# Feed-forward inner layer in two groups of tiles, x kept on chip at every post norm, other weight buffers, more layers in halves at the seams

## The chip, the cores and the metric

One core of a Trainium2 chip runs the whole network once. The metric is the device time of one execution in microseconds (us); lower is better. A time is the median of several runs.

## What is computed

x has 512 tokens of 1024 features. Four feed-forward layers, two attention-like mixers and two more mixers change it in turn, in the order feed-forward 0, attention, feed-forward 1, feed-forward 2, mLSTM, feed-forward 3, the even mixer, the odd mixer, and a last norm. Around the first six of these stand a norm before and a norm after (with a factor 0.5 in the gain of the feed-forwards' second norm):

```python
def _rms_norm(x, g):
    y = x * lax.rsqrt(jnp.mean(x * x, axis=-1, keepdims=True) + EPS)
    return y * g
def _swiglu(x, w_gate, w_up, w_down):
    return (jax.nn.silu(x @ w_gate) * (x @ w_up)) @ w_down
# feed-forward, D_FF = 2816:   x = x + 0.5 * _rms_norm(_swiglu(_rms_norm(x, g_pre), ...), g_post)
# attention and mLSTM:         x = x + _rms_norm(mixer(_rms_norm(x, g_pre)), g_post)
```

All of it is float32.

## The kernel before

**Layout and products.** Features lie on the partitions, tokens along the columns: x is 8 tiles of 128x512 (`k.x`). A float32 product is made of three products of reduced float32 (`mm3`, L287 to L289): each operand is split in a high and a low part, and low weights by high x, high weights by low x and high by high are added up in one PSUM bank. The three lines take a third of the matmuls each. `k.xs` holds the split x, which norm factors `rb` multiply later, behind the product.

**Weights.** `wload` (L260) brings a weight tile `wt` by DMA (128x1024, 512 KB), ScalarE makes the high part `wh` (L267, a cast), and VectorE the low part `wl` (L268, a subtraction); where `eng` is given, GpSimd does the subtraction. Each of the three has 4 buffers.

**Layers.** A `Lin` makes 128 output features for all 512 tokens. A feed-forward has 22 gate and 22 up layers (24 matmuls each), whose results become `hh` and `hl`, the 22 tiles of the inner layer, and then 8 down layers of 66 matmuls, for which all 22 tiles are on chip.

**Seams.** Between two parts of the network the norm needs every feature of a token. So the last layers of a part (`ntail`) and the first of the next one (`nfront`) run in two halves of 256 columns (`halves`, L316): the first half of the tokens goes through the post norm, the residual sum and the split while TensorE works on the second half of the last layers, and the second half while TensorE works on the first half of the next part. In the tail the second half goes backwards over its layers, and `tkeep` layers keep their weights; others are loaded twice. A tail's half is 2 layers in a feed-forward, 3 in the others; the front is 4 layers.

**The chain of a post norm** (`PostNorm`, L477 to L513). Of each layer ScalarE writes the squares to `ew` and the product times the gain to `hf`, which lies in the memory of x itself; GpSimd, for the last layer VectorE, adds the squares to `acc` (L493). Then two small matmuls sum over the partitions (L372), VectorE scales (`rsv`, L391), GpSimd takes the power -0.5 (L392), two small matmuls spread the result (L380), and for each of 8 tiles VectorE multiplies (L508) and adds the old x (L512, tiles 2 and 5 on GpSimd). The old x was copied to DRAM (`keep_x`, L465) and comes back by 8 DMAs for each half (L510). Behind it stand the split for the next part (ScalarE L433, VectorE L434), the squares of the new x (ScalarE L415, sums on GpSimd and VectorE L417, L419) and their column sums, scale, power and spread (`rc`), which give `rb`.

**What sets the order.** Chains are generators: `tick` advances them after so many matmul triples, so TensorE's place for each small matmul is fixed by numbers (`yield 3`, `lag=26`, 4 and 6 in `rsqrt_mean`); the tile scheduler then orders each engine's queue when the program is built. SP issues the DMAs in order. `ssm_prep` is side work for the even mixer that is spread over the gate and up layers of feed-forward 3; it begins with two DMAs into `pdt` (L1066) and an exponential on it (L1068).

Of the kernel before, what the change touches and what calls it, by code (L numbers as in the profile page):

```python
# [9 lines left out]
F32 = mybir.dt.float32  # L10
# [454 lines left out]
def keep_x(k):  # L465

    old = k.dram.tile([KX, P, T], F32, name="old", tag="old")
    for i in range(KX):
        k.nc.sync.dma_start(old[i], k.x[i])
    return old  # L470


class PostNorm:
# [3 lines left out]
    def __init__(s, k, gain, old):  # L477
        s.k, s.gain, s.hf, s.old = k, gain, hf_views(k.x), old
# [23 lines left out]
    def chain(s, c0, c1, then):  # L502
# [13 lines left out]
def ffn(k, w, gpost, side=None, begin=None):  # L516
# [3 lines left out]
    NB = 10  # L520
    with k.phase("ffn") as pool, k.psum("ffn_ps", True), ExitStack() as late:
        xs = k.xs
        hs = [(pool.tile([P, T], R, name=f"hh{i}"), pool.tile([P, T], R, name=f"hl{i}")) for i in range(NF - NB)]
# [24 lines left out]
        n1 = 2 * (NF - NB)  # L548
        if begin:
# [73 lines left out]
def attn(k):  # L623
# [3 lines left out]
    with k.phase("attn") as pool, k.psum("attn_ps") as pp:  # L627
# [9 lines left out]
        zero = pool.tile([P, T], F32, name="zero")  # L637
# [12 lines left out]
        def project(a, i):  # L650
# [26 lines left out]
            lins = [Lin(k, [(A["aqk"][2 * a + j, i], KX)], xs, ev, nc.gpsimd) for j, ev in ((1, ev_k), (0, ev_q))]  # L677
            if (a, i) != (0, 0):
                run_lins(lins)
            else:  # L680
# [4 lines left out]
                lin_tok(k, A["av"][0], xs, ev_v(0), nc.gpsimd)  # L685
# [76 lines left out]
        old = keep_x(k)  # L762
# [11 lines left out]
        post = PostNorm(k, k.vec(3), old)  # L774
        run_lins([Lin(k, [(A["ao"][m], KX)], ys, post.evac(m)) for m in range(KX)], ntail=3, on_half=post.finish)
# [5 lines left out]
def mlstm(k):  # L781
# [6 lines left out]
    with k.phase("mlstm") as pool, k.psum("mlstm_ps") as pp, ExitStack() as late:  # L788
# [11 lines left out]
        def gates(pa):  # L800
# [215 lines left out]
        post = PostNorm(k, k.vec(9), old)  # L1016
        run_lins([Lin(k, [(A["mo"][m], KX)], ys, post.evac(m)) for m in range(KX)], ntail=3, on_half=post.finish)
# [202 lines left out]
def even(k):  # L1220
# [3 lines left out]
    with k.phase("even") as pool, k.psum("even_ps") as pp:  # L1224
        xs, rb = k.xs, k.rb
        pwt = pool.tile([P, 4, P], F32, name="pwt")
        nc.sync.dma_start(pwt, A["pw"])
# [127 lines left out]
        for n, l in enumerate([None] + lus[2:] + lz[2:6] + lup + lz[6:], 1):  # L1355
# [237 lines left out]
```

## Time and profile before

| what | value |
|---|---|
| median of 3 runs | 2586.77 us (2586.46 to 2589.38) |
| the profiled execution's own time | 2588.2 us |
| its span, first to last instruction | 2586.4 us |
| its mean granted TensorE clock | 0.984 |
| busy: TensorE, VectorE, ScalarE, GpSimd | 95%, 53%, 39%, 25% |

The profile is one execution. TensorE's busy time is the sum of the time in which some matmul was under way; matmuls overlap each other, so their listed durations are longer than their steps from start to start. The granted clock is the share of TensorE's full clock that the chip let through.

### The profile page before, as it was taken

To read this page: it belongs to the slowest core of one execution; us is meant where nothing else is said; L and a number is where in the kernel's file an instruction comes from. 1 tells how busy PE (TensorE), PEld (TensorE's weight loads), DVE (VectorE), ACT (ScalarE), POOL (GpSimd) and SP (SyncE) were. 2 spreads that over 40 slices of the span, in tenths; PEclk is the share of its full clock that TensorE was granted. 3 is DMA by queue.
4 is the path that set the end of the run, shared out by engine and by line. 5 is a ranking of instruction groups with operands and counts; after the bars stand their busy time and mean duration, and the time that the engine had idled before them with its cause. 6 is when DMAs were issued, how large, how long until landed. Compare 5 with 4: busy or idle time off the path is not lost. (4 is left out here: it accounts for less than half of the span.)

```text
span 2586.4 us, 33337 instructions
## 1 busy us (share of the span) xinstructions
PE 2466.2 (95%) x12864; PEld 2071.5 (80%) x12864; DVE 1358.1 (53%) x2292; ACT 997.0 (39%) x1656; POOL 643.3 (25%) x566
## 2 busy tenths in 40 slices
PE   8999989999999999999999899979999999999898
PEld 7888887677888888888888788867888888787677
DVE  5443246656544432644422657449973245856884
ACT  4222234446522222422222445433232232346662
POOL 2111025030311100211100353122211014217961
PEclk9999999999999999999999999999999999999998
DMA  5223336122432333422233422224443347231111
GB/s 168 95 98 94 93 102 196 50 86 66 140 105 98 98 90 104 155 98 98 93 92 98 151 82 74 82 87 144 144 157 94 96 135 227 79 117 66 66 58 50
DMA packets 105679, 273.12 MB, mean 106 GB/s; under 512 B 17920, under 2 KB 39040, under 8 KB 105008
## 3 DMA queue, kind: packets, MB, share of 16 engines
q1 hardware_dynamic: 105520, 270.99, 33.1%
q8 instruction: 101, 1.65, 0.3%
q14 instruction: 58, 0.48, 0.1%
HBM read 243.66 MB, written 23.09 MB: 103 GB/s over the span
## 5 line engine op out<-in xcount | busy, mean ns | idle before, releaser
L287 PE MATMUL pa<-xs,wl 128*128 128x512 f32 (+1 forms) x2368 | 882.5, 373 | 9.2 <-DVE wl L268 7.1
L288 PE MATMUL pa<-xs,wh 128*128 128x512 f32 (+1 forms) x2368 | 881.7, 372 | 5.3 <-DVE xs L434 4.6
L289 PE MATMUL pa<-xs,wh 128*128 128x512 f32 (+1 forms) x2368 | 877.7, 371 | 0.0
L267 ACT CAST wh<-wt 128x1024 fp32r<-128x1024 f32 (+2 forms) x423 | 432.5, 1023 | 1048.8 <-issue 610.4
L268 DVE TENSOR_TENSOR wl<-wt,wh 128x1024 fp32r<-128x1024 f32 (+2 forms) x371 | 450.4, 1216 | 455.4 <-ACT wh L267 454.3
L287 PEld LDWEIGHTS pa<-xs,wl 128*128 128x128 f32 x2368 | 448.8, 190 | 87.4 <-ACT sq L415 7.1
L288 PEld LDWEIGHTS pa<-xs,wh 128*128 128x128 f32 x2368 | 448.5, 189 | 81.6 <-DVE xs L434 6.0
L289 PEld LDWEIGHTS pa<-xs,wh 128*128 128x128 f32 x2368 | 448.9, 190 | 74.3 <-issue 1.8
L533 POOL TENSOR_TENSOR ew<-ew,rb 128x512 f32<-128x512 f32 (+1 forms) x96 | 160.4, 1672 | 712.4 <-ACT ew L532 712.4
L287 PE MATMUL pa<-hh,wl 128*128 128x512 f32 (+1 forms) x880 | 311.6, 354 | 13.6 <-DVE wl L268 13.6
L288 PE MATMUL pa<-hl,wh 128*128 128x512 f32 (+1 forms) x880 | 309.6, 352 | 0.0
L289 PE MATMUL pa<-hh,wh 128*128 128x512 f32 (+1 forms) x880 | 309.6, 352 | 0.0
L287 PEld LDWEIGHTS pa<-hh,wl 128*128 128x128 f32 x880 | 167.6, 190 | 38.9 <-DVE wl L268 14.7
L493 POOL TENSOR_TENSOR acc<-acc,ew 128x512 f32<-128x512 f32 (+1 forms) x44 | 51.6, 1172 | 546.6 <-ACT ew L488 546.6
L288 PEld LDWEIGHTS pa<-hl,wh 128*128 128x128 f32 x880 | 167.6, 190 | 24.2
L289 PEld LDWEIGHTS pa<-hh,wh 128*128 128x128 f32 x880 | 167.5, 190 | 24.1
L540 DVE TENSOR_TENSOR ew<-ew,pa 128x512 f32<-128x512 f32 (+1 forms) x96 | 61.7, 643 | 227.8 <-PE pa L289 216.6
L531 DVE TENSOR_TENSOR ew<-rb,pa 128x512 f32<-128x512 f32 (+1 forms) x96 | 61.4, 642 | 177.9 <-PE pa L289 175.2
L268 POOL TENSOR_TENSOR wl<-wt,wh 128x1024 fp32r<-128x1024 f32 x52 | 126.4, 2443 | 110.3 <-ACT wh L267 110.1
L1454 POOL TENSOR_TENSOR tp<-tp 128x512 f32<-128x512 f32 x72 | 100.0, 1389 | 5.1 <-ACT tp L1450 0.7
L1461 DVE SCALAR_TENSOR_TENSOR pc<-g,vecs,pc 128x512 f32<-128x512 f32 x120 | 85.8, 751 | 4.4 <-PE pc L1459 3.4
L488 ACT ACTIVATE ew<-pa 128x512 f32<-128x512 f32 (+1 forms) x56 | 27.3, 488 | 138.8 <-PE pa L289 138.8
(457 smaller groups left out, 2851.8 us busy)
## 6 DMA issues: line engine op xcount, KB each, us to landing
wt<-in_wgu_dram SPq DMA_DIRECT2D x176, 512.0 KB, 3.5
wt<-in_wd_dram SPq DMA_DIRECT2D x72, 512.0 KB, 3.5
wt<-in_wd_dram SPq DMA_DIRECT2D x36, 384.0 KB, 3.1
wt<-in_ow_dram SPq DMA_DIRECT2D x24, 512.0 KB, 3.3
old<-x SPq DMA_DIRECT2D x40, 256.0 KB, 3.3
old<-old SPq DMA_DIRECT2D x80, 128.0 KB, 2.3
wt<-in_aqk_dram SPq DMA_DIRECT2D x18, 512.0 KB, 4.2
wt<-in_mvo_dram SPq DMA_DIRECT2D x16, 512.0 KB, 3.8
```

Source lines behind the costliest of these rows:

```text
L267: nc.scalar.copy(wh, wt)
L268: (eng or nc.vector).tensor_tensor(wl, wt, wh.bitcast(F32), op=ALU.subtract)
L287: mm(ps[:m, c0:c1], wl[:, j, :], xh[:, c0:c1], start=first and j == 0, stop=False)
L288: mm(ps[:m, c0:c1], wh[:, j, :], xl[:, c0:c1], start=False, stop=False)
L289: mm(ps[:m, c0:c1], wh[:, j, :], xh[:, c0:c1], start=False, stop=last and j == n - 1)
L488: nc.scalar.activation(sq[:, c0:c1], ps[:, c0:c1], AF.Square)
L493: eng.tensor_tensor(s.acc[:, c0:c1], s.acc[:, c0:c1], sq[:, c0:c1], op=ALU.add)
L531: nc.vector.tensor_tensor(s[:, c0:c1], rb[:, c0:c1], ps[:, c0:c1], op=ALU.mult)
L533: nc.gpsimd.tensor_tensor(s[:, c0:c1], s[:, c0:c1], rb[:, c0:c1], op=ALU.mult)
L540: nc.vector.tensor_tensor(s[:, c0:c1], s[:, c0:c1], ps[:, c0:c1], op=ALU.mult)
L1454: nc.gpsimd.tensor_tensor(part, part, t, op=ALU.add)
L1461: nc.vector.scalar_tensor_tensor(ps, gi[:, j:j + T], cw[:, at[j]:at[j] + 1], ps, op0=ALU.mult, op1=ALU.add)
```

## The change

- Weight buffers: `wt` 3, `wh` and `wl` 5 each (4 each before).
- Post norms: the product goes to tiles of its own (feed-forward: new tiles; attention and mLSTM: memory that is free by then), x stays where it is, and the chain adds to it in place. The copy of x to DRAM and the DMAs back are gone. The gain is applied in the chain's multiplication.
- Feed-forward: gate and up layers 0 to 11, then the down layers over these 12 tiles (8 layers of 36 matmuls, copied to `hf`), then gate and up layers 12 to 21 into the same inner tiles, then the down layers over these 10 (30 matmuls each), which VectorE adds to `hf` before ScalarE squares it.
- Halves: tail of 4 layers in the feed-forwards (2 layers keep their weights), 5 in attention and mLSTM; front of 6 layers, but for the first feed-forward.
- Lags of the norm factors: 28 and 38 triples, and 9 for the power. The side work of feed-forward 3 starts one layer later.
- Attention: the low weights of the first group are made by VectorE instead of GpSimd; `zero` shares memory with `gr`. mLSTM: the gate layer runs in two halves with two token blocks between them. Even mixer: `pwt` is loaded later.

Counted over the built programs, TensorE gets 240 matmuls of 512 columns split in two of 256, and 48 the other way.

```diff
 def wload(k, src, shape, eng=None):
-    wt = k.wp.tile(shape, F32, name="wt", tag="wt", bufs=4)
+    wt = k.wp.tile(shape, F32, name="wt", tag="wt", bufs=3)
-    wh = k.wp.tile(shape, R, name="wh", tag="wh", bufs=4)
-    wl = k.wp.tile(shape, R, name="wl", tag="wl", bufs=4)
+    wh = k.wp.tile(shape, R, name="wh", tag="wh", bufs=5)
+    wl = k.wp.tile(shape, R, name="wl", tag="wl", bufs=5)
...
-    prs = yield from rsqrt_mean(k, t, c0, c1, 1024, 1e-6, 6, v)
+    prs = yield from rsqrt_mean(k, t, c0, c1, 1024, 1e-6, 9, v)
...
-def prenorm(k, g, c0, c1, lag=26, order=range(KX)):
+def prenorm(k, g, c0, c1, lag=None, order=range(KX)):
+    lag = lag or (28 if c0 == 0 else 38)
...
-            nc.scalar.activation(sq[:, c0:c1], ps[:, c0:c1], AF.Square)
-            nc.scalar.activation(s.hf[m][:, c0 // HALF:c1 // HALF, :], ps[:, c0:c1].rearrange("p (a t) -> p a t", t=HALF),
-                                 AF.Copy, scale=s.gain[:, m:m + 1])
+            hf = s.hf[m][:, c0:c1]
+            if s.add:
+                nc.vector.tensor_tensor(hf, hf, ps[:, c0:c1], op=ALU.add)
+                nc.scalar.activation(sq[:, c0:c1], hf, AF.Square)
+            else:
+                nc.scalar.activation(sq[:, c0:c1], ps[:, c0:c1], AF.Square)
+                nc.scalar.copy(hf, ps[:, c0:c1])
...
-            nc.vector.tensor_tensor(tmp[:, c0:c1], s.hf[i][:, c0 // HALF, :], prs[:, c0:c1], op=ALU.mult)
-            x = k.sm.tile([P, HALF], F32, name="old", tag="old", bufs=3)
-            nc.sync.dma_start(x, s.old[i, :, c0:c1])
+            nc.vector.scalar_tensor_tensor(tmp[:, c0:c1], s.hf[i][:, c0:c1], s.gain[:, i:i + 1], prs[:, c0:c1],
+                                           op0=ALU.mult, op1=ALU.mult)
             eng = nc.gpsimd if i in (2, 5) else nc.vector
-            eng.tensor_tensor(k.x[i][:, c0:c1], x, tmp[:, c0:c1], op=ALU.add)
+            eng.tensor_tensor(k.x[i][:, c0:c1], k.x[i][:, c0:c1], tmp[:, c0:c1], op=ALU.add)
...
 def ffn(k, w, gpost, side=None, begin=None):
+        nf = 4 if begin else 6
+        run_lins(lins[:nf], nfront=nf)
...
-        run_lins(lins[n1:])
-        post = PostNorm(k, gain, old)
...
-        run_lins(lins, ntail=2, on_half=post.finish, tkeep=1)
+        run_lins([down(m, 0, NA, ev_part(m)) for m in range(KX)])
+        run_lins(lins[n1:])
+        post = PostNorm(k, gain, hf, True)
+        run_lins([down(m, NA, NF, post.evac(m)) for m in range(KX)], ntail=4, on_half=post.finish, tkeep=2)
+        k.need("xs", 0, T)
...
-            lins = [Lin(k, [(A["aqk"][2 * a + j, i], KX)], xs, ev, nc.gpsimd) for j, ev in ((1, ev_k), (0, ev_q))]
+            eng = None if (a, i) == (0, 0) else nc.gpsimd
+            lins = [Lin(k, [(A["aqk"][2 * a + j, i], KX)], xs, ev, eng) for j, ev in ((1, ev_k), (0, ev_q))]
...
-        post = PostNorm(k, k.vec(3), old)
-        run_lins([Lin(k, [(A["ao"][m], KX)], ys, post.evac(m)) for m in range(KX)], ntail=3, on_half=post.finish)
+        post = PostNorm(k, k.vec(3), [hf[m // 4][:, m % 4, :] for m in range(KX)])
+        run_lins([Lin(k, [(A["ao"][m], KX)], ys, post.evac(m)) for m in range(KX)], ntail=5, on_half=post.finish)
```

**Order on VectorE, second part of the chain of the first half, end of feed-forward 1** (`ew` the product by the norm factor, `x_91` to `x_98` the eight tiles of x, `xs` the split, `old` the x read back). Before:

```order
L512 TENSOR_TENSOR x_97<-old,ew 128x256
L512 TENSOR_TENSOR x_98<-old,ew 128x256
L434 SCALAR_TENSOR_TENSOR xs_103<-x_95,vecs,xs_103 128x256
L434 SCALAR_TENSOR_TENSOR xs_104<-x_96,vecs,xs_104 128x256
L268 TENSOR_TENSOR wl<-wt,wh 128x1024
L417 TENSOR_TENSOR ssq<-ssq,sq 128x256
L434 SCALAR_TENSOR_TENSOR xs_105<-x_97,vecs,xs_105 128x256
L417 TENSOR_TENSOR ssq<-ssq,sq 128x256
L434 SCALAR_TENSOR_TENSOR xs_106<-x_98,vecs,xs_106 128x256
L419 TENSOR_TENSOR ssq<-ssq 128x256
L268 TENSOR_TENSOR wl<-wt,wh 128x768
```

Changed (`hf` the product of the down layers, `pa` its PSUM bank):

```order
L429 SCALAR_TENSOR_TENSOR xs_105<-x_97,vecs,xs_105 128x256
L414 TENSOR_TENSOR ssq<-ssq 128x256
L429 SCALAR_TENSOR_TENSOR xs_106<-x_98,vecs,xs_106 128x256
L478 TENSOR_TENSOR hf_6895<-hf_6895,pa 128x256
L478 TENSOR_TENSOR hf_6894<-hf_6894,pa 128x256
L478 TENSOR_TENSOR hf_6893<-hf_6893,pa 128x256
L263 TENSOR_TENSOR wl<-wt,wh 128x640 x2
L386 TENSOR_SCALAR rc<-pb 128x2
L263 TENSOR_TENSOR wl<-wt,wh 128x1024
```

The weight subtraction inside the chain is gone from it; the two of the tail's last layer stand behind the whole chain and behind three additions to `hf`.

**Order on ScalarE, mLSTM to feed-forward 3**, from the last evacuations of the mLSTM's tail to the squares of the second half (`pa` a PSUM bank, `rb` the norm factors of the first half). Before:

```order
L488 ACTIVATE ew<-pa 128x256
L489 ACTIVATE x_96<-pa,vecs 128x256
L267 CAST wh<-wt 128x1024
L1068 ACT_TABLE_LOAD
L1068 ACTIVATE pdt<-pdt 128x16
L415 ACTIVATE ssq<-x_91 128x256
L433 ACTIVATE xs_99<-x_91,vecs 128x256
```

Changed:

```order
L482 COPY vx<-pa 128x256
L262 CAST wh<-wt 128x1024
L446 COPY rb<-pb 128x256
L1074 ACT_TABLE_LOAD
L1074 ACTIVATE pdt<-pdt 128x16
L410 ACTIVATE ssq<-x_91 128x256
L410 ACTIVATE sq<-x_92 128x256
```

The exponential on `pdt` stands ahead of the second half's squares in both; in the change the copy of `rb` is ahead of it.

**Order on GpSimd, feed-forward 0 to attention.** Before:

```order
L512 TENSOR_TENSOR x_96<-old,ew 128x256
L493 TENSOR_TENSOR acc<-acc,ew 128x256
L268 TENSOR_TENSOR wl<-wt,wh 128x1024 x2
L392 TENSOR_TENSOR rc<-rc,mhalf 128x2
L268 TENSOR_TENSOR wl<-wt,wh 128x1024
```

Changed:

```order
L503 TENSOR_TENSOR x_96<-x_96,ew 128x256
L485 TENSOR_TENSOR acc<-acc,ew 128x256 x3
L387 TENSOR_TENSOR rc<-rc,mhalf 128x2
L387 TENSOR_TENSOR rsv<-rsv,mhalf 128x2
L503 TENSOR_TENSOR x_93<-x_93,ew 128x256
```

The weight subtractions are gone from this place, and three additions of squares stand where one stood.

## Rows read from the trace of the kernel before

**Rows 1.** The page: busy us by engine; costliest groups: count, busy us, mean ns, idle.

```profile
PE 2466.2 (95%) x12864; PEld 2071.5 (80%) x12864; DVE 1358.1 (53%) x2292; ACT 997.0 (39%) x1656; POOL 643.3 (25%) x566
...
L268 DVE TENSOR_TENSOR wl<-wt,wh 128x1024 fp32r<-128x1024 f32 (+2 forms) x371 | 450.4, 1216 | 455.4 <-ACT wh L267 454.3
```

**Rows 2.** Waits of TensorE, whole span: total us, times, longest us.

```profile
PE pb L380 <- POOL rc L392: 24.3, 9, 18.7
PE pa L287 <- DVE wl L268: 24.2, 6, 7.4
PE pb L372 <- DVE ssq L419: 11.3, 3, 5.2
```

**Rows 3.** Busy time by window: length; PE, PEld, DVE, ACT, POOL; clock, DMA share, GB/s.

```profile
360.00:410.00 50.00, 39.59 (x273) 36.48 (x272) 32.06 (x57) 20.79 (x44) 25.00 (x22) 0.90 0.38 119
640.00:710.00 70.00, 64.03 (x426) 57.94 (x425) 38.36 (x80) 37.10 (x75) 20.98 (x23) 0.98 0.39 128
1040.00:1090.00 50.00, 43.57 (x330) 42.35 (x330) 34.54 (x79) 24.73 (x53) 14.21 (x16) 0.93 0.50 159
1400.00:1460.00 60.00, 52.60 (x358) 48.22 (x357) 36.03 (x75) 26.05 (x53) 16.19 (x25) 0.95 0.52 161
1700.00:1760.00 60.00, 37.97 (x280) 36.39 (x279) 34.30 (x108) 25.46 (x60) 17.75 (x26) 0.83 0.34 109
2100.00:2160.00 60.00, 56.00 (x431) 53.96 (x430) 36.63 (x79) 26.08 (x54) 16.93 (x16) 0.97 0.64 206
```

**Rows 4.** Timeline of VectorE, feed-forward 0 to attention: start, us, engine, line.

```profile
376.14 0.75 DVE L512 TENSOR_TENSOR x<-old,ew 128x256 f32<-128x256 f32 x2
376.81 3.44 DVE L434 SCALAR_TENSOR_TENSOR xs<-x,vecs,xs 128x256 fp32r<-128x256 f32 x2
```

**Rows 5.** Timeline of GpSimd in the same stretch.

```profile
376.07 1.41 POOL L493 TENSOR_TENSOR acc<-acc,ew 128x256 f32<-128x256 f32 x1 [1.59 <-ACT ew L488]
377.44 5.01 POOL L268 TENSOR_TENSOR wl<-wt,wh 128x1024 fp32r<-128x1024 f32 x2
```

**Rows 6.** Timeline of ScalarE, mLSTM to feed-forward 3; in brackets the idle time before.

```profile
1738.92 1.28 ACT L1068 ACT_TABLE_LOAD   x1 [18.03 <-DMA pdt<-in_ldt_dram]
...
1740.34 0.40 ACT L415 ACTIVATE ssq<-x 128x256 f32<-128x256 f32 x1
```

**Rows 7.** DMA issues of that stretch: count, KB each, median us to landing.

```profile
pdt<-in_ldt_dram SPq DMA_DIRECT2D x2, 4.0 KB, 17.1
```

**Rows 8.** Timeline of SP's queue: issue of these two.

```profile
1716.37 1.37 SPq L1066 DMA_DIRECT2D pdt<-in_ldt_dram  x2
```

**Rows 9.** Timeline of TensorE: first and last of unbroken stretches of one shape.

```profile
99.67 0.39 PE L287 MATMUL pa<-xs,wl 128*128 128x512 f32 x1
...
103.98 0.39 PE L288 MATMUL pa<-xs,wh 128*128 128x512 f32 x1
```

**Rows 10.** The same for 256 columns, split x, then the inner tiles.

```profile
29.80 0.28 PE L287 MATMUL pa<-xs,wl 128*128 128x256 f32 x1
...
33.88 0.28 PE L288 MATMUL pa<-xs,wh 128*128 128x256 f32 x1
...
1023.92 0.28 PE L287 MATMUL pa<-hh,wl 128*128 128x256 f32 x1
...
1030.44 0.28 PE L288 MATMUL pa<-hl,wh 128*128 128x256 f32 x1
```

**Rows 11.** Timeline of VectorE, feed-forward 1 to 2, the chain of the second half.

```profile
1066.34 0.75 DVE L508 TENSOR_TENSOR ew<-x,pb 128x256 f32<-128x256 f32 x2 [1.58 <-PE pb L380]
...
1070.40 0.43 DVE L512 TENSOR_TENSOR x<-old,ew 128x256 f32<-128x256 f32 x1 [0.51 <-DMA old<-old]
1071.28 0.43 DVE L512 TENSOR_TENSOR x<-old,ew 128x256 f32<-128x256 f32 x1 [0.45 <-DMA old<-old]
...
1074.65 0.43 DVE L417 TENSOR_TENSOR ssq<-ssq,sq 128x256 f32<-128x256 f32 x1 [1.08 <-ACT sq L415]
...
1077.52 0.42 DVE L419 TENSOR_TENSOR ssq<-ssq 128x256 f32<-128x256 f32 x1
```

More of the change, by code (lines that the diff above doesn't have):

```diff
@@ L462, in prenorm, with __init__ @@
     return work()
[L465 to L470, printed above, removed]
 class PostNorm:
-    def __init__(s, k, gain, old):
-        s.k, s.gain, s.hf, s.old = k, gain, hf_views(k.x), old
+    def __init__(s, k, gain, hf, add=False):
+        s.k, s.gain, s.hf, s.add = k, gain, hf, add
         s.acc, s.done = None, {a: [] for a, b in HALVES}
@@ L519, in ffn @@
     nc = k.nc
-    NB = 10
+    NA = 12
     with k.phase("ffn") as pool, k.psum("ffn_ps", True), ExitStack() as late:
         xs = k.xs
-        hs = [(pool.tile([P, T], R, name=f"hh{i}"), pool.tile([P, T], R, name=f"hl{i}")) for i in range(NF - NB)]
+        hs = [(pool.tile([P, T], R, name=f"hh{i}"), pool.tile([P, T], R, name=f"hl{i}")) for i in range(NA)]
         gain = k.sm.tile([P, KX], F32, name="gain", tag="gain")
@@ L558, in ffn @@
             k.spawn(norm_factor(k, *HALVES[1], 42), *HALVES[1])
-            old = k.A["xT"].rearrange("(i p) t -> i p t", p=P)
         rb = k.rb
-        run_lins(lins[:4], nfront=4)
-        if not begin:
-            old = keep_x(k)
+        nf = 4 if begin else 6
+        run_lins(lins[:nf], nfront=nf)
         if side:
@@ L566, in ffn @@
                 work = side(k, sp)
-                for l in lins[4:n1]:
+                for n, l in enumerate(lins[nf:n1]):
                     run_lins([l])
-                    next(work, None)
+                    if n:
+                        next(work, None)
                 for _ in work:
@@ L636, in attn @@
         r8 = pool.tile([P, 2, 4], F32, name="r8")
-        zero = pool.tile([P, T], F32, name="zero")
+        zero = pool.tile([P, T], F32, name="zero", tag="gr", bufs=1)
         nc.gpsimd.memset(zero, 0.0)
@@ L761, in attn @@
         k.need("all", 0, T)
-        old = keep_x(k)
         for j, f in enumerate((0.125, -0.125)):
@@ L773, in attn @@
             hilo(k, yf[i], ys[i], 0, T)
-        post = PostNorm(k, k.vec(3), old)
-        run_lins([Lin(k, [(A["ao"][m], KX)], ys, post.evac(m)) for m in range(KX)], ntail=3, on_half=post.finish)
+        hf = [pool.tile([P, 4, T], F32, name=f"hf{a}", tag=f"vt{a}") for a in range(2)]
+        post = PostNorm(k, k.vec(3), [hf[m // 4][:, m % 4, :] for m in range(KX)])
+        run_lins([Lin(k, [(A["ao"][m], KX)], ys, post.evac(m)) for m in range(KX)], ntail=5, on_half=post.finish)
+        k.need("xs", 0, T)
 LAG, QK = 1, 2
@@ L826, in gates @@
             gw = wload(k, A["mg"], [P, KX, 64])
-            pg = k.A_()
-            for c in HALVES:
-                mm3(k, pg, gw, xs, *c)
+            pg = k.S_()
+            mm3(k, pg, gw, xs, *HALVES[0])
+            yield
+            mm3(k, pg, gw, xs, *HALVES[1])
             nc.vector.tensor_tensor(gs, rb[:64], pg[:64], op=ALU.mult)
@@ L875, in mlstm @@
         lv = [LinTok(k, A["mvo"][a], xs, ev_v(a), nc.gpsimd if a else None) for a in range(2)]
-        for tb in range(4):
+        for tb in range(2):
             lv[0].run(tb)
-        k.need("all", 0, T)
-        old = keep_x(k)
         with k.phase("mlstm_a") as pa:
             gt = gates(pa)
+            next(gt)
+            for tb in range(2, 4):
+                lv[0].run(tb)
+            k.need("all", 0, T)
             next(gt)
@@ L1015, in mlstm @@
             gated(h)
-        post = PostNorm(k, k.vec(9), old)
-        run_lins([Lin(k, [(A["mo"][m], KX)], ys, post.evac(m)) for m in range(KX)], ntail=3, on_half=post.finish)
+        vf = vx.rearrange("p c h d -> p (c h d)")
+        post = PostNorm(k, k.vec(9), [vf[:, m * T:(m + 1) * T] for m in range(KX)])
+        run_lins([Lin(k, [(A["mo"][m], KX)], ys, post.evac(m)) for m in range(KX)], ntail=5, on_half=post.finish)
+        k.need("xs", 0, T)
 def cmul(nc, tmp, o_re, o_im, ar, ai, br, bi, eng=None, sub=None):
@@ L1225, in even @@
         xs, rb = k.xs, k.rb
-        pwt = pool.tile([P, 4, P], F32, name="pwt")
-        nc.sync.dma_start(pwt, A["pw"])
+        pwt = []
         inv = pool.tile([P, 4, 16], F32, name="inv")
@@ L1335, in mix @@
             pm = pp.tile([P, T], F32, name="pe", tag="E")
-            mm(pm, pwt[:, i, :], pl, start=True, stop=True)
+            mm(pm, pwt[0][:, i, :], pl, start=True, stop=True)
             nc.vector.scalar_tensor_tensor(pl, pm, k.vecs[:, C_PS + i:C_PS + i + 1], sz[i], op0=ALU.mult, op1=ALU.mult)
@@ L1360, in even @@
                 next(parts[i])
+            if n == 6:
+                pwt.append(pool.tile([P, 4, P], F32, name="pwt", tag="u", bufs=4))
+                nc.sync.dma_start(pwt[0], A["pw"])
             if n < 10:
```

24 lines of the change are left out of this document (13 added, 11 removed).

## The prediction

> **What bounds the kernel now.** I read the page first: TensorE is busy 2466.2 of 2586.4 us, and no other engine is above 53% [rows 1]. So time comes only from TensorE: from its idle stretches, from the stretches at half clock, or from the number of its steps. The list of TensorE's waits then says who ends the idle time: the norm factor's power `rc` (24.3 us, one wait of 18.7), weights whose low part isn't ready (24.2, longest 7.4) and sums of squares (11.3) [rows 2]. All of these stand at the seams. The table by stage shows six seams that the change touches [rows 3]; the reader should add the idle time (length minus PE busy) and (1 - clock) times length: 15.4, 7.4, 9.9, 10.4, 32.2 and 5.8 us, together 81. Counted finer, each matmul against the step of its shape [rows 9, 10], I get 15.8 (feed-forward 0 to attention), 11.8 (attention to feed-forward 1), 12.3 (1 to 2), 12.0 (2 to mLSTM), 28.4 (mLSTM to 3) and 9.4 (3 to even), together 89.7. That is what the change can win; the steps of all other matmuls stay.
>
> Two places need a closer look. At 376 two of VectorE's splits take 3.44 us, the two additions just ahead of them 0.75 [rows 4], and GpSimd makes two weight subtractions in 5.01 meanwhile [rows 5]; the weight for which TensorE waits 7.4 us stands behind these splits on VectorE. At 1739 ScalarE has stood 18.03 us in front of the exponential on `pdt`, whose two 4 KB DMAs had a median of 17.1 us to landing and were issued at 1716 to 1718 [rows 6 to 8]: the later landed some 22 us after its issue, the earlier after some 12. The squares of the second half stand behind the exponential, so `rc` came 18.7 us late.
>
> **The change part by part.**
>
> *Steps.* 240 matmuls of 512 columns become 480 of 256, and 48 go the other way. The unbroken stretches give 4.31/19 = 0.2268 us for a step of 512 [rows 9] and 4.08/34 = 0.1200 for one of 256 [rows 10], so a split costs 0.0132 and 240 cost 3.2 us; I leave out what the 48 give back. Below, nothing; above, the listed lengths 2 x 0.28 - 0.39 = 0.17 for each, 41 us, but those overlap, so I take **+3.2**.
>
> *x on chip.* The copies and the 80 DMAs back go. The chain of the second half ran from 1066.34 to 1077.94, 11.6 us, with 0.51 and 0.45 of waiting for the old x and 1.08 for squares [rows 11]. Without these 9.6; the multiplication with the gain reads one operand more, some 0.06 us on each of 8, so **10.1 us** for a chain with nothing else in it. In the first half a weight subtraction stood in the chain and is behind it now.
>
> *Tails of the feed-forwards.* A half is now 4 layers of 30 matmuls at 6.52/55 = 0.1185 [rows 10], 14.2 us; before, 2 of 66, 15.7. So the cover got 1.5 us shorter while the chain got about as much shorter. From the start of the second half: the sums, the power and the spread take about 4.0 (lags of 3 and 4 triples of 0.36, and 1.58 in which VectorE waited for the spread [rows 11]), then 10.1 of chain: the sums of squares stand at 14.1. By the order TensorE comes to their column sums after 90 matmuls, at 10.7, plus 1.2 for the small products and the wait for the power: 11.9. It waits **2.2**. Then the tail's last layer needs its low weights, which stand on VectorE behind the chain and behind three additions to `hf` (from 14.1: three additions 1.0, the last split 0.4, and 0.76 for a 128x640 tile, by 640/1024 of 1216 ns [rows 1]; the few matmuls left of the layer before cover 0.6): **1.55** more. Such short stops still cost clock: the seam at 1040 lost 0.07 x 50 = 3.5 in two dips [rows 3], so **1.8** for one. Tail: 5.6 us. In the same finer count the four tails lost 11.0, 5.3, 2.0 and 4.7 before, together 23.0; 4 x 5.6 = 22.4. The tails win nothing.
>
> *Fronts.* Six layers instead of four give the second half's chain a cover of 6 x 24 x 0.12 = 17.3 us. (i) Feed-forward 0 to attention: GpSimd's weight subtractions go, and the 7.4 us with them; in their place TensorE waits about 3.3 for the first half's sums of squares (the attention's first layers are shorter cover) and 0.8 for a weight, with 0.9 of power waits and 1.8 of clock. With the tail 12.5, **-3.3**. (ii) Attention to feed-forward 1: tail of 5 x 24 x 0.12 = 14.4 covers the chain's end at 14.1; what remains is 3.3 for the last sum into `acc` (weight casts stand ahead of the last square on ScalarE), clock 2.0 and some 1.6 of powers: 6.9, **-4.9**. (iii) Feed-forward 1 to 2: power waits 1.2, a weight behind the second chain 1.7, clock 1.8, with the tail 10.5: **-1.8**. (iv) Feed-forward 2 to mLSTM: the gate layer's weights stand behind the second chain, 4.1, with clock 2.2 and 1.0 of powers: 12.9, **+0.9**. (v) mLSTM to feed-forward 3: in the new order the exponential on `pdt` still stands ahead of the second half's squares; its DMAs are issued 18 to 20 us after the tail's second half began, so with the 22 that the slower of the pair needed before, TensorE stands about 16 us there, and 3.2 at `acc`: with clock 24.4, **-4.0**. (vi) Feed-forward 3 to even: 8.0, **-1.4**. Sum of the seams **-14.5**.
>
> Here a rule bears on (v). The DMAs of `pdt` had a median of 17.1 us for 4 KB [rows 7]. The Trainium skill, page "DMA: Bandwidth & Descriptors", section "Bandwidth", has 0.68 us of transfer for 4 KB (and calls small transfers descriptor-dominated); by it, as an estimate, `pdt` would be there before ScalarE comes to it and the 16 us would go. The row is of these very DMAs, so it decides the sum.
>
> *At no cost.* Copying the first group's product (8 copies for each feed-forward, on a ScalarE that is 39% busy [rows 1]), 8 additions on VectorE (53%) and the switches between the groups lie beside whole layers; if their cover went, a switch would show as one wait of a weight, 4.0 us by the list's mean (24.2/6) [rows 2], and two more switches in each of four feed-forwards make 32 us as upper end; I take nothing, since no switch from up to down layers waits in the trace of before. Three `wt` buffers in place of four: while VectorE is in a chain, SP can bring 3 tiles, and 5 finished pairs cover 2.5 layers in a feed-forward's tail; this is in the 1.55. Even's `pwt`, `zero` and the gates' halves: nothing, hidden by project layers.
>
> Sum: +3.2 - 14.5 = -11.3 from the profiled execution's 2588.2, 2576.9. The median lies 1.4 below that execution, so the forecast against 2586.8 is **2576**, bounds on its own 2569 to 2582.
>
> **The rivals.**
>
> *B, the stops get too short for the clock to fall, or `pdt` lands in time.* For: 24.9 of the 81 us are clock [rows 3], and seams with less idle time lose less of it. The Trainium skill, page "TensorE: Matmul & The Clock Gate", section "Part 1: The HAM clock gate", says that idling, not load, throttles the array; the rows agree in that 0.83 goes with the longest stop and 0.97 and 0.98 with the shortest. If the six dips of about 1.8 go, 11 less: 2565. If `pdt` is in time, 16 less: 2560. Against: 2.2 and 1.55 stand close together, and the order still has `pdt` first. Time: **2562**.
>
> *C, stalls only move.* Each wait removed shows the next one behind it: the seams keep their length, and the splits stay: 2586.8 + 3, less the 2 to 4 us of memory waits that surely go: **2587**.
>
> *D, slower: GpSimd's additions stretch the chain.* The tails now make three additions of squares on GpSimd for each half where one stood, and the chains on VectorE run beside them. At 376 VectorE's two splits took 3.44 us beside a GpSimd instruction [rows 4, 5]; but the two additions at 376.14 took 0.75 beside GpSimd's addition to `acc`, which took 1.41 itself. The Trainium skill, page "SBUF — State Buffer", section "Who interferes with whom", says that a VectorE instruction with two SBUF inputs and a GpSimd one that reads SBUF exclude each other, the later waiting for the whole of the earlier; rows 4 fit it in one place and not in the other. As a mechanism of this kernel: two more additions x 1.41 in a chain that is already 2.2 late make TensorE wait 2.8 more at each of six seams, 17 us: 2593, and with the weights behind the chain a little more, **2594**. It decides from 1.9 us a chain (11.3/6). Against: on GpSimd the additions stand behind its two additions of x, so late in the chain.
>
> That the change doesn't do what it says is no case: the order shows the DMAs gone and the layers split.
>
> **How the numbers follow.** The forecast has 0.42, B 0.20, C 0.21, D 0.17. A measurement tells 0.2% from no change, 5.2 us: faster is below 2581.6, slower above 2592. Faster: B and nearly all of the forecast's own range, 0.60. Same: C, with the forecast's upper edge and D's lower part, 0.25. Slower: most of D, 0.15. The range for 8 in 10 reaches to 2556, past B, and to 2593, to D's middle; C lies inside.
>
> **What would show it.** Right: DMA rows of `old` gone; TensorE's wait on weights from 24.2 to near 12, without the 7.4; a wait on sums of squares of about 2 at each of four tails; one wait on sums or `rc` of about 16 at mLSTM to 3; steps of 0.2268 and 0.1200 as before; GpSimd no longer beside stretched splits. Wrong: no wait at the tails and clock near 1 there (B), a `pdt` that lands within a few us (B), weight waits longer than 3 us at the tails or chains longer than 12 us (D), new waits inside the feed-forwards at the switches.

## The result, and the profile after

The changed kernel takes 2625.4 us (median of 4 runs, 2619.1 to 2628.0) against 2588.1 of the kernel before beside it: ratio 1.014, interval 1.012 to 1.016. It is **slower by 37 us** where 11 us faster was forecast (2576 against 2586.8). Its profiled execution took 2619.1 us, the fastest of the four, with a span of 2617.1, 30.7 more than before; so the traces show some 31 of the 37 us.

The waits of TensorE after the change (total us, times, longest), to be read beside [rows 2]:

```profile
PE pb L367 <- DVE ssq L414: 30.5, 8, 13.4
PE pa L282 <- DVE wl L263: 20.0, 8, 7.5
...
PE pe L1300 <- POOL xx L1293: 8.2, 2, 4.3
...
PE pa L282 <- ACT hf L482: 5.6, 2, 4.9
PE pb L375 <- POOL rc L387: 5.5, 4, 2.1
...
PE pa L282 <- ACT vx L482: 4.9, 1, 4.9
PE pa L349 <- DVE vx L873: 4.1, 1, 4.1
```

The waits on `rc` fell from 24.3 to 5.5, and those on sums of squares rose from 11.3 to 30.5: the same stop at mLSTM to feed-forward 3, 13.4 us, now ends at another instruction. Waits of about 4 us or more that are new: two on `xx` of the even mixer, two of 4.9 us on copies by ScalarE, `hf` and `vx`, and one of 4.1 on a copy by VectorE, also to `vx`, at feed-forward 2 to mLSTM. The stages, with the columns of [rows 3]; the last is the even mixer:

```profile
360.00:430.00 70.00, 60.90 (x361) 53.65 (x360) 45.98 (x94) 29.14 (x59) 20.14 (x23) 0.90 0.31 98
640.00:720.00 80.00, 72.94 (x533) 67.50 (x530) 43.73 (x86) 39.75 (x84) 23.97 (x26) 0.96 0.23 74
1043.00:1103.00 60.00, 50.54 (x387) 49.07 (x386) 42.38 (x89) 28.06 (x59) 18.29 (x20) 0.94 0.29 94
1426.00:1500.00 74.00, 62.64 (x364) 54.92 (x363) 42.13 (x85) 31.29 (x58) 28.96 (x33) 0.93 0.30 93
1712.00:1785.00 73.00, 52.92 (x383) 51.86 (x382) 42.76 (x124) 34.85 (x74) 20.98 (x29) 0.84 0.19 55
2126.00:2180.00 54.00, 48.07 (x379) 46.75 (x379) 38.98 (x83) 25.30 (x54) 18.32 (x18) 0.97 0.46 156
2180.00:2300.00 120.00, 106.51 (x505) 87.39 (x504) 87.31 (x97) 30.09 (x41) 48.28 (x30) 0.94 0.43 136
```

The even mixer before, same view:

```profile
2150.00:2270.00 120.00, 111.82 (x566) 92.05 (x565) 82.89 (x102) 33.37 (x45) 50.38 (x32) 0.99 0.46 143
```

By the prediction's rough measure, idle time plus (1 - clock) times length, the six seams lose 63.0 + 32.3 = 95 us (81 before) and the even mixer 13.5 + 7.2 = 21 (9 before). The seams were to give and took; the even mixer, for which the prediction took nothing, lost 11 more. In the finer count (matmul by matmul) the seams lose 18.2, 15.1, 15.7, 18.5, 29.0 and 10.1, in sum 107 against 90, and the even mixer about 9 more than before.

### The profile page after: what moved, and what is told of

It is laid out like the page before. It is cut to its first block, busy times and chain, and to the rows that moved or that the text cites. A ratio compares the mean times of both kernels' runs of the same rounds, so it can differ in the third digit from the quotient of the medians.

```text
span 2617.1 us, 33783 instructions
## 1 busy us (share of the span) xinstructions
PE 2481.6 (95%) x13056; PEld 2093.5 (80%) x13056; DVE 1414.2 (54%) x2401; ACT 1014.3 (39%) x1717; POOL 638.4 (24%) x573
## 3 DMA queue, kind: packets, MB, share of 16 engines
q1 hardware_dynamic: 92272, 251.58, 30.7%
## 5 line engine op out<-in xcount | busy, mean ns | idle before, releaser
L282 PE MATMUL pa<-xs,wl 128*128 128x512 f32 (+1 forms) x2424 | 894.9, 369 | 18.3 <-DVE wl L263 9.6
L283 PE MATMUL pa<-xs,wh 128*128 128x512 f32 (+1 forms) x2424 | 891.9, 368 | 1.2 <-DVE xs L1380 0.6
L284 PE MATMUL pa<-xs,wh 128*128 128x512 f32 (+1 forms) x2424 | 889.6, 367 | 0.0
L262 ACT CAST wh<-wt 128x1024 fp32r<-128x1024 f32 (+3 forms) x467 | 446.2, 958 | 1043.0 <-issue 485.8
L263 DVE TENSOR_TENSOR wl<-wt,wh 128x1024 fp32r<-128x1024 f32 (+3 forms) x423 | 479.1, 1135 | 370.8 <-ACT wh L262 366.1
L282 PEld LDWEIGHTS pa<-xs,wl 128*128 128x128 f32 x2424 | 463.6, 191 | 91.8 <-ACT sq L410 7.5
L283 PEld LDWEIGHTS pa<-xs,wh 128*128 128x128 f32 x2424 | 463.5, 191 | 74.0 <-DVE xs L1380 2.5
L284 PEld LDWEIGHTS pa<-xs,wh 128*128 128x128 f32 x2424 | 463.3, 191 | 72.9 <-issue 2.8
L283 PEld LDWEIGHTS pa<-hl,wh 128*128 128x128 f32 x864 | 166.3, 192 | 24.9 <-issue 0.2
L485 POOL TENSOR_TENSOR acc<-acc,ew 128x256 f32<-128x256 f32 (+1 forms) x56 | 57.2, 1022 | 335.6 <-ACT ew L479 172.6
L263 POOL TENSOR_TENSOR wl<-wt,wh 128x1024 fp32r<-128x1024 f32 x44 | 108.0, 2465 | 118.6 <-ACT wh L262 118.5
L349 PE MATMUL pa<-wh,xs 128*128 128x512 f32 x176 | 70.9, 404 | 5.3 <-DVE vx L873 4.1
```

Source lines behind the costliest of these rows:

```text
L282: mm(ps[:m, c0:c1], wl[:, j, :], xh[:, c0:c1], start=first and j == 0, stop=False)
L283: mm(ps[:m, c0:c1], wh[:, j, :], xl[:, c0:c1], start=False, stop=False)
L284: mm(ps[:m, c0:c1], wh[:, j, :], xh[:, c0:c1], start=False, stop=last and j == n - 1)
L349: mm(ps, xl[:, t], wh[:, i % 2, :], start=i == 0, stop=False)
L485: eng.tensor_tensor(s.acc[:, c0:c1], s.acc[:, c0:c1], sq[:, c0:c1], op=ALU.add)
```

## The experiments

Times are medians; "before" lay between 2587 and 2589 beside all of them. A diff is against the change where nothing else is said.

**Groups of 8 and 14.** More cover in the tails.

```diff
-    NA = 12
+    NA = 8
...
```

The second group then has 14 tiles, so six inner tiles are added to the first group's eight.

> The change with groups of 8 and 14 tiles instead of 12 and 10, so each down layer of the tail has 42 matmuls and a half of the tail lasts 4 x 42 x 0.1185 = 19.9 us instead of 14.2. Theory A (the cover of the feed-forward tails is too short: at each of four tails TensorE waits 2.8 us for the sums of squares and 1.9 for the last layer's low weights, and the clock falls behind it): these waits go, 4 x (4.7 + about 2 of clock) = 27 us less than the change's 2625, so 2595 to 2608. Theory B (the loss is elsewhere, in the even mixer and in the tails of the mixers, from the deeper weight buffers and the tail of 5): no more than 6 us less.

Measured 2632.6. The side work in feed-forward 3 had too few layers left: TensorE waited there 18.3 and 4.0 us for copies to `hf`, and 9.3 at its start for a product by VectorE. The run says nothing clean of the tails, so it was repeated with `NA = 12 if side else 8`:

> The change with groups of 8 and 14 tiles in feed-forwards 0 to 2, and 12 and 10 as in the change in feed-forward 3, whose side work has too few layers left with 8 (in groups_8_14 TensorE stood there 18.3 and 4 us). Theory A (cover of the tails): 3 tails x about 6 = 12 to 20 us below the change, 2605 to 2613. Theory C (the tail's stops only move: the sums of squares come in time, but the last layer's weights still wait behind the chain and the last sum into acc and the front's sums come later instead): within 6 us of the change.

Measured 2614.8, 10.6 below the change, between the two. In feed-forward 1's tail and the front behind it, the change first and then this run:

```profile
1062.12 0.68 PE L367 MATMUL pb<-ones,ssq 128*128 128x128 f32 x4 [2.80 <-DVE ssq L414]
...
1064.68 0.58 PE L282 MATMUL pa<-hh,wl 128*128 128x256 f32 x1 [1.88 <-DVE wl L263]
...
1086.07 0.68 PE L367 MATMUL pb<-ones,ssq 128*128 128x128 f32 x4 [1.57 <-DVE ssq L414]
...
1088.56 0.58 PE L282 MATMUL pa<-xs,wl 128*128 128x256 f32 x1 [1.81 <-DVE wl L263]
```

```profile
1049.64 0.68 PE L367 MATMUL pb<-ones,ssq 128*128 128x128 f32 x4 [0.57 <-DVE ssq L414]
...
1052.01 0.39 PE L282 MATMUL pa<-hh,wl 128*128 128x256 f32 x1 [1.68 <-DVE wl L263]
...
1066.12 0.70 PE L367 MATMUL pb<-ones,acc 128*128 128x128 f32 x4 [1.91 <-DVE acc L485]
...
1081.31 1.20 PE L367 MATMUL pb<-ones,ssq 128*128 128x128 f32 x4 [3.40 <-DVE ssq L414]
```

The wait for the sums falls from 2.80 to 0.57 us with 19.9 us of cover, that for the last layer's weight stays (1.88, now 1.68), and the two behind it grow from 1.57 and 1.81 to 1.91 and 3.40: the four come to 7.6 us in place of 8.1, so here the stop only moved, as Theory C has it. The 10.6 us are 3.5 a tail on the average, where Theory A wanted about 6; more of them came at feed-forward 2 to mLSTM, where the wait of 4.1 us on `vx` is gone.

**Buffers 4/4/4.** The same for `wl` as for `wh`.

```diff
-    wt = k.wp.tile(shape, F32, name="wt", tag="wt", bufs=3)
+    wt = k.wp.tile(shape, F32, name="wt", tag="wt", bufs=4)
...
-    wh = k.wp.tile(shape, R, name="wh", tag="wh", bufs=5)
+    wh = k.wp.tile(shape, R, name="wh", tag="wh", bufs=4)
```

> The change with 4 buffers each for wt, wh and wl. Theory B1 (with 5 pairs GpSimd's weight subtractions stand ahead of the even mixer's xx, which then comes late and stretches VectorE's instructions): the waits of 4.3 and 3.9 us on xx shrink to below 1.5 and the even mixer, which lost 10 us more than before, gives back 8 to 10: about 2616; the rest unchanged. Theory A: the even mixer's loss is not from the buffers, and the tails of the feed-forwards get worse by one pair less: 2625 to 2640.

Measured 2611.3, **14.2 below** the change. The waits on `xx` come to 0.3 us together (8.2 in the change), and in the finer count the even mixer gives back about 7 of the 9 us that it lost, although TensorE now waits 4.3 us there for a product by VectorE. B1 holds for the place; the run changes buffers everywhere, so the cause was taken alone later. `gp` is the engine of the even mixer's weight subtractions:

```diff
-        gp = nc.gpsimd
+        gp = nc.vector
```

> The change, with the weight subtractions of the even mixer's layers on VectorE instead of GpSimd and the buffers 3/5/5 kept. Theory B1 in its narrow form (the loss in the even mixer is GpSimd's subtractions that stand in front of xx and stretch VectorE's instructions beside them): the waits of 4 us on xx go and the even mixer gives back 5 to 9 us, 2616 to 2620. If VectorE has no room there (it makes the scans and products of the same chain): no change or slower. If the loss comes from another effect of the buffers, the even mixer still loses 8 to 10.

Measured 2612.9, **12.5 below** the change with the buffers kept, more than was expected; no wait of TensorE on `xx` is left, and the even mixer loses 0.7 us less than before. So some 10 of the 12.5 us are the even mixer's own; the rest is not placed. The narrow form holds. GpSimd in the change, in the even mixer:

```profile
2189.34 6.59 POOL L263 TENSOR_TENSOR wl<-wt,wh 128x1024 fp32r<-128x1024 f32 x2
2197.21 1.29 POOL L1290 TENSOR_TENSOR xx<-r 128x512 f32<-128x512 f32 x1 [1.28 <-issue]
2198.47 2.36 POOL L263 TENSOR_TENSOR wl<-wt,wh 128x1024 fp32r<-128x1024 f32 x1
2202.05 1.27 POOL L1293 TENSOR_TENSOR xx<-r 128x512 f32<-128x512 f32 x1 [1.23 <-DVE r L1292]
```

VectorE in the change, in the same stretch:

```profile
2193.66 2.82 DVE L1288 TENSOR_TENSOR r<-r,rot 128x512 f32<-128x512 f32 x1
2196.40 0.68 DVE L1289 TENSOR_TENSOR r<-r,rot 128x512 f32<-128x512 f32 x1
2198.54 2.83 DVE L1291 TENSOR_TENSOR r<-r,rot 128x512 f32<-128x512 f32 x1 [1.46 <-POOL xx L1290]
```

The same instructions of VectorE, before and then with the subtractions on VectorE (there with GpSimd's first `xx`):

```profile
2167.33 0.66 DVE L1283 TENSOR_TENSOR r<-r,rot 128x512 f32<-128x512 f32 x1
...
2170.06 0.69 DVE L1286 TENSOR_TENSOR r<-r,rot 128x512 f32<-128x512 f32 x1 [1.47 <-POOL xx L1285]
```

```profile
2197.72 1.21 DVE L263 TENSOR_TENSOR wl<-wt,wh 128x1024 fp32r<-128x1024 f32 x1
2197.92 2.16 POOL L1290 TENSOR_TENSOR xx<-r 128x512 f32<-128x512 f32 x1 [4.39 <-issue]
2200.12 0.69 DVE L1291 TENSOR_TENSOR r<-r,rot 128x512 f32<-128x512 f32 x1 [1.19 <-POOL xx L1290]
```

With a fifth pair of buffers GpSimd may subtract one weight earlier, and the scheduler put it ahead of `xx`: two subtractions before the first `xx` and one between the two, where before there was one and none. A VectorE product that takes 0.68 us took 2.82 beside a subtraction, and TensorE waited 3.9 and 4.3 us for `xx`. That the fifth pair of `wh` and `wl`, and not the third `wt`, made the difference was not tried apart.

**Tails of 3 in the mixers.** In attention, and the same in mLSTM:

```diff
-    run_lins([Lin(k, [(A["ao"][m], KX)], ys, post.evac(m)) for m in range(KX)], ntail=5, on_half=post.finish)
+    run_lins([Lin(k, [(A["ao"][m], KX)], ys, post.evac(m)) for m in range(KX)], ntail=3, on_half=post.finish)
```

> The change with tails of 3 layers instead of 5 in attention and mLSTM. Theory B2 (with 5 layers TensorE runs into the squares and splits of the chain on ScalarE, which stand ahead of the copies that free its PSUM banks: two waits of 4.9 us on hf and vx): both go, with the clock behind them 7 to 12 us less, 2613 to 2618. Theory A (the cover decides): a shorter tail (8.6 us) uncovers the chain of about 14, and the wait moves into the last sums or the front: no change or up to 10 us slower.

Measured 2609.4, **16.0 below** the change. Both waits of 4.9 us are gone, as B2 says. In the change's attention tail, TensorE and then ScalarE:

```profile
680.10 0.58 PE L282 MATMUL pa<-xs,wl 128*128 128x256 f32 x1 [4.92 <-ACT hf L482]
```

```profile
673.30 0.41 ACT L410 ACTIVATE ssq<-x 128x256 f32<-128x256 f32 x1
...
677.53 1.69 ACT L428 ACTIVATE xs<-x,vecs 128x256 fp32r<-128x256 f32 x4
679.12 0.36 ACT L481 ACTIVATE ew<-pa 128x256 f32<-128x256 f32 x1
...
679.70 0.35 ACT L482 COPY hf<-pa 128x256 f32<-128x256 f32 x1
```

The squares and splits of the chain, from 673.3 on, stand ahead of the evacuation at 679.1, and its copy to `hf` at 679.7 frees the bank that TensorE's next layer needs. At attention the gain is given back in the next front (in the finer count about 7 less in attention, 8 more in feed-forward 1): with the tail of 3 TensorE waits 2.8 us for a split and then for `rc`.

```profile
702.43 1.23 PE L375 MATMUL pb<-ident,rc 128*128 128x128 f32 x4 [4.93 <-POOL rc L387]
```

At mLSTM it stays, because with the shorter tail SP reaches `pdt`'s DMAs some 18 us earlier, counted from the end of the tail (22 on the clock of the trace), and the exponential no longer waits. This seam loses some 14 us less, so most of the gain is the stop on `pdt`. SP in the change and in this run, then ScalarE in the change:

```profile
1737.01 0.66 SPq L1072 DMA_DIRECT2D pdt<-in_ldt_dram  x1
...
1739.62 0.63 SPq L1072 DMA_DIRECT2D pdt<-in_ldt_dram  x1
```

```profile
1715.38 1.62 SPq L1072 DMA_DIRECT2D pdt<-in_ldt_dram  x2
```

```profile
1760.39 1.28 ACT L1074 ACT_TABLE_LOAD   x1 [14.78 <-DMA pdt<-in_ldt_dram]
...
1761.80 0.40 ACT L410 ACTIVATE ssq<-x 128x256 f32<-128x256 f32 x1
```

**Fronts of 4** and the old lags.

```diff
-        nf = 4 if begin else 6
+        nf = 4
...
-    lag = lag or (28 if c0 == 0 else 38)
+    lag = lag or 26
...
-    prs = yield from rsqrt_mean(k, t, c0, c1, 1024, 1e-6, 9, v)
+    prs = yield from rsqrt_mean(k, t, c0, c1, 1024, 1e-6, 6, v)
```

> The change with the fronts and lags as they were: 4 layers in halves, lags of 26 and 6 triples. If the longer fronts cover the second half's chain, as was predicted, this is slower by 5 to 15 us (2630 to 2640), with waits on sums of squares in the fronts. If the longer lags are a cost of the change (rc and rb later, evacuations waiting), it is faster by 3 to 8 us.

Measured 2618.7, 6.7 below the change; but its profiled execution, 2619.9 of span, is 3 above the change's. Alone it settles little, so the fronts were compared without the other two losses (bufs_4_tails_3 joins the first two diffs, combo all three):

> The change with buffers 4/4/4 and mixer tails of 3, but its long fronts and lags. Alone 14 and 16 us: if independent, 2595. Since combo (fronts of 4 as well) took 2593.4, this tells what the fronts and lags are worth without the stop on pdt: 2600 if they cost 7 as they did alone, 2585 to 2592 if they are a gain once that stop is gone, as predicted.

> The change with all three undone at once: buffers 4/4/4, tails of 3 in the mixers, fronts of 4 with the old lags. Alone these gave 14, 16 and 7 us. If they are independent, 2625 - 37 = 2588, level with the kernel before: then x on chip and the two groups are worth nothing in sum. If the gains overlap (the same stop, ended by different waits), 2595 to 2605; if x on chip does shorten the chains once these waits are gone, below 2582.

Measured 2599.6 with the long fronts and lags and 2593.4 without (9 runs, 2592.4 to 2596.5). The fronts and lags cost 6 us with or without the stop on `pdt`. Most of it lies inside feed-forward 3, not at the seams. Its side work is spread over the layers between the front and the end of the first group, 18 with a front of 6 and 20 with one of 4. TensorE in bufs_4_tails_3:

```profile
1894.26 1.28 PE L1175 MATMUL pb<-pz,pbb 128*32 128x128 f32 x32 [2.83 <-ACT pout L1168]
...
1931.01 0.51 PE L282 MATMUL pa<-hh,wl 128*128 128x512 f32 x1 [1.41 <-ACT hf L569]
```

Neither wait is there in combo. Counted matmul by matmul, feed-forward 3's inside loses some 7 us more with the long front, the seams together some 2 less, and 144 more split matmuls cost 1.9 at 0.0132 each [rows 9, 10]. Fronts and lags were not tried apart.

14.2 and 16.0 make 30 alone and 25.8 together, so they overlap a little. With all three undone 6 us remain over the kernel before (ratio 1.0025, interval 1.0014 to 1.0035): what is left of the change is worth less than nothing.

**`pdt` in feed-forward 0**, on the kernel before: its DMAs go out behind the third inner tile, on ScalarE's queue.

```diff
+            k.pdt = k.const.tile([P, 16], F32, name="kpdt")
+            nc.vector.tensor_copy(k.pdt, hs[2][0][:, 0:16].bitcast(F32))
...
+                nc.scalar.dma_start(k.pdt[gg * 64:(gg + 1) * 64, :], ld[gg:gg + 1, :].to_broadcast([64, 16]))
...
-    nc.scalar.activation(dt, dt, AF.Exp)
+    nc.scalar.activation(dt, k.pdt, AF.Exp)
```

> The kernel before with the two DMAs of pdt issued in feed-forward 0, 1700 us earlier, so that the exponential waits for nothing. If this wait alone makes the 18.7 us stop on rc at mLSTM to feed-forward 3: 16 to 24 us less than before (with the half clock behind it), 2565 to 2573. If another wait stands right behind it (sums of squares, weights behind the chain), 5 to 12 less.

Measured 2573.4, ratio 0.995 (0.9935 to 0.9965): **14 us less**, a little under the first range, since a wait for `rc` of 4.9 us remains at 1735:

```profile
1735.29 1.22 PE L380 MATMUL pb<-ident,rc 128*128 128x128 f32 x4 [4.93 <-POOL rc L392]
```

> The run combo with pdt loaded in feed-forward 0 as well. If the stop on pdt is independent of the change, 13 to 20 us less than combo. If in the change the stop at this seam is set by the chain and its weights too, less than 8.

Measured 2592.4, 1 below combo: with tails of 3 the DMAs land in time anyway. The kernel before has tails of 3 too, but there the eight DMAs of the old x stand ahead of `pdt`'s in SP's order:

```profile
1708.54 7.31 SPq L510 DMA_DIRECT2D old<-old  x8
```

It issues `pdt`'s 1.1 us before the tail's end, combo 18.7. So at this seam combo loses some 14 us less than the kernel before, as before_pdt does. That it is x on chip that brings `pdt` forward is read from the order and was not tried alone.

**VectorE for attention's first weights**, on the kernel before, as in the change.

```diff
-            lins = [Lin(k, [(A["aqk"][2 * a + j, i], KX)], xs, ev, nc.gpsimd) for j, ev in ((1, ev_k), (0, ev_q))]
+            eng = None if (a, i) == (0, 0) else nc.gpsimd
+            lins = [Lin(k, [(A["aqk"][2 * a + j, i], KX)], xs, ev, eng) for j, ev in ((1, ev_k), (0, ev_q))]
...
-                lin_tok(k, A["av"][0], xs, ev_v(0), nc.gpsimd)
+                lin_tok(k, A["av"][0], xs, ev_v(0))
```

> The kernel before with the low weights of attention's first group (two layers and the first token layer) made by VectorE instead of GpSimd, nothing else. Prediction's own term: the wait of 7.4 us at 376 and the half clock behind it go, 3 to 10 us less, 2578 to 2585. If VectorE, which does the chains there, becomes the one that is late: no change.

Measured 2584.0, ratio 0.9986 (0.9976 to 0.9995): a gain of 3.5 us, at the small end. TensorE's wait of 7.4 us on the weight became one of 2.9 on a weight and one of 3.4 on `rc`.

**x on chip in the mixers alone**, on the kernel before with `pdt` early; `PostNormX` is the change's class. Attention, and likewise mLSTM:

```diff
-        old = keep_x(k)
...
-        post = PostNorm(k, k.vec(3), old)
+        hf = [pool.tile([P, 4, T], F32, name=f"hf{a}", tag=f"vt{a}") for a in range(2)]
+        post = PostNormX(k, k.vec(3), [hf[m // 4][:, m % 4, :] for m in range(KX)])
```

> before_pdt with x on chip in attention and mLSTM alone: the change's chain (gain in the multiplication, x added in place, no DMAs of the old x) with the old tails of 3, the old fronts and buffers, the feed-forwards untouched. If a chain without waits for the old x is worth what was predicted (1 to 2 us for each of two seams): 2 to 5 below before_pdt's 2573.4. If the DMAs were hidden anyway: 2572 to 2575. If the changed chain is itself slower (three operands, ScalarE's order): 2 to 5 above.

Measured 2578.1, 4.6 above before_pdt, with no overlap between the runs of the two (2575.9 to 2579.3, and 2572.3 to 2575.7): the third case. TensorE's waits at attention to feed-forward 1:

```profile
679.63 0.38 PE L288 MATMUL pa<-xs,wh 128*128 128x256 f32 x1 [2.95 <-DVE xs L434]
...
701.99 1.22 PE L380 MATMUL pb<-ident,rc 128*128 128x128 f32 x4 [3.41 <-POOL rc L392]
```

In before_pdt these waits are 0.29 + 1.96 and 0.46 us. Which of the chain's edits makes the splits and `rc` later was not tried apart.

**Best of each.**

> The run combo_pdt with groups of 8 and 14 tiles in feed-forwards 0 to 2. Theory A: 12 to 20 us below combo_pdt's 2592, so 2572 to 2580, level with before_pdt. Theory C: 2586 to 2595.

Measured 2592.9, level with combo_pdt: the longer tails bring nothing once the other losses are gone; Theory A falls.

> The kernel before with pdt loaded in feed-forward 0 and the low weights of attention's first group on VectorE. Alone these gave 14 and 3.5 us; they lie 1300 us apart, so if they are independent 2587.5 - 17 = 2570.5. This would be the fastest version so far.

Measured **2568.6** (5 runs, 2567.5 to 2570.2), ratio 0.9929 (0.9917 to 0.9941): the fastest version, 57 us below the change and 19 below the kernel before, with x still read back from DRAM.

## Why the prediction was wrong

The sum gave the seams -14.5 us and the steps +3.2. In the finer count the seams came to +17, each of the six above its forecast: 18.2, 15.1, 15.7, 18.5, 29.0 and 10.1, where 12.5, 6.9, 10.5, 12.9, 24.4 and 8.0 were forecast. The even mixer came to +9 and the inside of feed-forward 3 to +5, and for neither had anything been taken.

- **"At no cost ... Three `wt` buffers in place of four ... this is in the 1.55"** is the first step that failed. The prediction looked at the buffers in the tails alone. What they did was to let GpSimd's subtractions run earlier in the even mixer, a part that it held to be untouched: 12.5 us by even_on_vector. The mechanism, a GpSimd instruction that stretches VectorE's, was named as rival D and put in the wrong place.
- **"Tail of 5 x 24 x 0.12 = 14.4 covers the chain's end"** is the second. The cover was counted in TensorE's time alone, not in PSUM banks: what frees a bank stands behind the chain on ScalarE, 4.9 us twice, and seam (ii) lost 15.1 where 6.9 was forecast. The tail also kept `pdt`'s DMAs back, so that mixer_tails_3 gains 16 us; but that stop was in the forecast of (v), and taking the 4.9 us away gained nothing at attention.
- **"Six layers instead of four give the second half's chain a cover"** is the third. The cover was worth some 2 us at the seams. Its price was not counted: two layers less for the side work of feed-forward 3, some 7 us there, and with the splits a loss of 6 (bufs_4_tails_3 against combo).
- **"The gate layer's weights stand behind the second chain, 4.1"** came out in size, but by luck: the 4.1 us at feed-forward 2 to mLSTM are a wait for a PSUM bank. VectorE's copy to `vx`, which frees it, stands behind the second half's chain, as ScalarE's copies do at the mixers:

```profile
1470.57 1.40 DVE L873 TENSOR_SCALAR vx<-pa,rc 128x512 f32<-128x512 f32 x2
```

- **"Without these 9.6 ... 10.1 us for a chain"** was right in size and wrong in worth. In the change the chain of feed-forward 1's first half ran from 1051.33 to 1061.97, 10.6 us, but the mixers with it were 4.6 slower than without. Taking away the 1 us of waiting for the old x gained nothing there.
- **The tails of the feed-forwards** went nearly as worked out: 2.80 us for the sums (2.2 forecast) at three of the four, 0.86 at feed-forward 2, and 1.57 to 1.89 for the weight (1.55) at all four. There GpSimd's additions do stretch VectorE, but behind the chain: two subtractions of 128x640 took 2.62 us beside them, where one took 0.83 with nothing beside it (at 1050.58). Feed-forward 1's tail, the chain's first and last instruction on VectorE and what follows, with GpSimd's additions:

```profile
1051.33 0.87 DVE L500 SCALAR_TENSOR_TENSOR ew<-hf,gain,pb 128x256 f32<-128x256 f32 x2
...
1061.55 0.42 DVE L414 TENSOR_TENSOR ssq<-ssq 128x256 f32<-128x256 f32 x1
...
1062.28 1.08 DVE L478 TENSOR_TENSOR hf<-hf,pa 128x256 f32<-128x256 f32 x3
1063.22 3.26 POOL L485 TENSOR_TENSOR acc<-acc,ew 128x256 f32<-128x256 f32 x3 [6.68 <-ACT ew L479]
1063.28 2.62 DVE L263 TENSOR_TENSOR wl<-wt,wh 128x640 fp32r<-128x640 f32 x2
```

- **The clock** was under-priced: the seven stages lose 39.5 us to it by the rough measure, 26 before (24.9 by [rows 3] and 1.2 in the even mixer). The idle time of these stages grew by 12 us (64 to 76) and the loss to the clock by 13, so the new stops cost about as much again in granted clock (0.84 to 0.97 in these stages).
- **The stop on `pdt`** was right: 13.4 us against 16 forecast, and the order, not the exponential's length, decides it. **Splits**: the steps came out at about 2 us more against 3.2; the 48 that go the other way had been left out. **GpSimd's weights in attention**: the 7.4 us wait went, but two others stood behind it, and alone the edit is worth 3.5.

The three losses (buffers 14, tails 16, fronts and lags 6) come to 32 together, from 2625.4 to 2593.4. The 6 us that remain are not all that the rest of the change costs, since combo has lost the stop on `pdt` and has VectorE for attention's first weights. With both in the kernel before as well, 24 us lie between the two (combo_pdt 2592.4, before_pdt_dve 2568.6). x on chip in the mixers is 4.6 of them. The other 19 are spread over the feed-forwards' seams, feed-forward 2 to mLSTM most, and the even mixer, and which edit makes them stays open. In combo_pdt TensorE waits 4.2 to 4.3 us for sums of squares at three of the four feed-forward tails:

```profile
1058.08 1.19 PE L367 MATMUL pb<-ones,ssq 128*128 128x128 f32 x4 [4.25 <-DVE ssq L414]
```

## What to carry to other kernels

Count what a deeper buffer lets run earlier on every engine that fills it, over the whole program, and not only where it was wanted: the scheduler puts it in front of something. A cover is as long as the scarcest thing that it needs, and banks, the queue that empties them and the DMA queue behind it count as much as matmuls. A transfer of a few KB in single elements belongs long before its use; here that was worth 14 us, more than anything that the change tried. Layers lent to one stretch are taken from another: two more in the front were two fewer for the side work.

## What had not been expected of the hardware

A VectorE product with two SBUF operands took 2.83 us in place of 0.68 when it began 0.07 us after a GpSimd subtraction of 2.36 us. With the order turned round, GpSimd's `xx` took 2.16 us in place of 1.29 when it began 0.2 us after a subtraction by VectorE, which kept its 1.21. So the one that begins later pays. This agrees with the rule of the Trainium skill's page "SBUF — State Buffer", section "Who interferes with whom", that the later one waits. The prediction took [rows 4, 5] to fit it in one place only. They fit it in both: GpSimd's addition at 376.07, which takes 0.74 us where nothing runs beside it (at 357.08), took 1.41, and a sum on VectorE (375.80, 0.42 us) had begun before it.

The two 4 KB DMAs of `pdt` took a median of 14.2 us in the change as well, and 17.8 in before_pdt, where ScalarE issued them and not SP. The traces show them as some 2,000 packets of four bytes, which go out at about 107 a microsecond in the kernel before and in before_pdt, and a little more slowly in the change. What sets this rate is not shown.
